# All products of x as seven block products per pair of tiles, with the work of attention and RG-LRU placed beside the gates

## The chip, the cores and the metric

One core of a Trainium2 chip. The metric is the device time of the whole kernel in microseconds (us), from a few runs. Engines are called PE (TensorE), DVE (VectorE), ACT (ScalarE), POOL (GpSimd) and SP (SyncE, which issues the DMAs).

## The reference

One layer of a streaming encoder on x of 1024 tokens x 1024 channels, float32:

```
h = x @ w_in                                  # 46 column tiles of 128
y_a = rglru(conv(xa)) * gelu(ya)              # 8 tiles of h
y_b = b_gate * conv(c_gate * xh)              # 12 tiles
y_c = rwkv7(z)                                # 14 tiles: r, k, v, two low-rank inputs, one gate input
y_d = chunk_attention(q, k, v, rel_bias)      # 12 tiles, 8 heads of 64
merged = sum over n of sigmoid(x @ w_gate[n] + b_gate[n]) * (y[n] @ w_branch[n])   # 32 gate tiles
x = layer_norm(ALPHA * x + merged @ w_out)
ff = square(relu(x @ w_ff1)) @ w_ff2
x = layer_norm(ALPHA * x + ff + (p @ w_ple) * sigmoid(x @ w_ple_gate + b_ple_gate))
```

## The kernel before, in words

**Arithmetic.** Operands are split into a high and a low part of a reduced type. Gemm.split casts on ACT (line 347, the high part) and subtracts on DVE (line 348, the low part). Gemm.acc issues three matmuls per 128 rows of the contraction, high x high, low x high and high x low (lines 367, 368, 369), each 128x512 into a bank of PSUM.

**Products of x.** gemm_x makes one column tile: Gemm.load fetches its weights as one [128, 1024] tile and splits them in two halves; for each half of the tokens 8 x 3 matmuls run, so 48 per tile. x is split once, at the start (xh, xl). Its users are generators: zc_tile (RWKV inputs, stored to zs in DRAM), qkv_tile (stored to qkv), lru, sconv, and gate or spill (tanh of a gate tile; spill also stores it to gsd). ff1 and the embedding's gate already run in another form, seven, after combine has built sums of the blocks of x1: two column tiles are taken as a 2 x 2 block product of seven block products (12 matmuls each), with the sums of weight blocks on POOL (lines 1074, 1097, 1098).

**Order.** Instructions are recorded in the order of the code; work under tc.high_priority is moved ahead. The RWKV part is a chain of 16 units (two halves of the channels, 8 chunks of 128 tokens), Rwkv.unit, each a long sequence of small matmuls with an eviction or an elementwise step between them: pn, pq, ptm, ptv, pw, then pt and py in turn (lines 231 and 246, the copy YT on ACT between them), p12, px, pss, pp, po. After each unit, run(oth, n) records n half tiles of other products (NO = 5 per unit, NOB = 6 for the first), which fill PE between the steps; issue_after holds them behind the mark of a unit LAG = 2 back. A unit loads its inputs from zs into zt (line 115, 10 x 128 columns, two buffers); "inv" on ACT (line 128) is among the first to read it.

lru and sconv lie among these fillers. After the units come three spilled gates, then for n = 0 to 3 the gates and branch products, with attend giving steps of attention at high priority: one beside a gate already in gsd, three beside a gate computed there, times NA = 1.6. One step of attention is 14 small matmuls (scores p, transposes pt, values po), two reductions on DVE (lines 761, 766), an exponential (line 771) and copies on ACT (line 783). Then w_out with the first norm, x1_transposed and combine, the embedding, ff1, and ff2 with the last norm.

## Time and profile before

| | |
|---|---|
| runs | 2408.91, 2410.81, 2416.87 us; median 2410.81 |
| profiled execution | 2414.82 us, its span 2413.0 us |
| PE, DVE, ACT, POOL busy | 98%, 56%, 35%, 14% of the span |
| matmuls | 12114 |
| mean granted clock of PE | 0.99 |
| stages, by their first matmul | the units' step p12 (line 259) from 225 (unit 0) to 977 us (unit 15), branches and attention from 1041, w_out from 1514, x1 transposed and combined from 1580, embedding 1623, ff1 1740, ff2 2053 to the end |

A row of the windows view gives for a stretch the busy time of each engine with its count of instructions, the granted clock of PE, the busy share of the DMA engines and what they moved. Starts and durations of matmuls overlap in the records, so the number of matmuls in a window says more than their busy time. A row of the groups names line, engine, operation, output and inputs, shapes and count, then busy time and the mean of one in ns, then the idle time ahead of them and what ended it.

### The profile page before, as it was taken

What the parts mean: (1) busy time and instruction counts of PE and PEld (TensorE: products, weight loads), DVE (VectorE), ACT (ScalarE), POOL (GpSimd) and SP (SyncE); (2) the same over time, 40 slices, a digit from 0 to 9 for tenths busy, and PEclk for the clock granted to TensorE, in tenths of its full rate; (3) what the DMA queues carried; (4) which work ended last, traced back from release to release, by engine and by line L of the source; (5) the groups of instructions that cost most, each with busy time, mean ns of one, the idle gap of its engine ahead of it and who ended that gap; (6) DMA issues with size and microseconds to landing.
All of it is one profiled execution on the core that took longest, in us unless ns stands there. A gap on an engine that the chain in (4) does not pass through costs nothing.

```text
span 2413.0 us, 31988 instructions
## 1 busy us (share of the span) xinstructions
PE 2369.2 (98%) x12114; PEld 1951.1 (81%) x12114; DVE 1353.1 (56%) x2758; ACT 845.9 (35%) x1478; POOL 345.2 (14%) x310
## 2 busy tenths in 40 slices
PE   9999999999999999999999999997999999999998
PEld 7888788777777778878888888876888888888886
DVE  5354545677677642245534334777644444776667
ACT  5543322424334222234434343334344444321110
POOL 0000100010000100000211100114145555000001
PEclk9999999999999999999999999998999999999999
DMA  5532222112121112254512224401123333532311
GB/s 200 192 126 70 88 71 70 56 53 66 53 71 53 64 60 77 98 174 125 158 53 73 80 76 142 164 31 57 44 96 111 112 114 130 187 123 89 103 53 70
DMA packets 123850, 231.33 MB, mean 96 GB/s; under 512 B 20016, under 2 KB 51888, under 8 KB 123696
## 3 DMA queue, kind: packets, MB, share of 16 engines
q1 hardware_dynamic: 123696, 229.29, 28.4%
q8 instruction: 95, 1.56, 0.3%
q14 instruction: 59, 0.48, 0.1%
HBM read 169.48 MB, written 59.77 MB: 95 GB/s over the span
## 4 chain that ended last, share of the span: by engine, by line
PE 91%; DVE 3%; DMA 3%; ACT 1%; issue 1%; POOL 0%; SPq 0%; DVEq 0%; ACTq 0%; POOLq 0%
PE f L368 5%; PE f L367 5%; PE f L369 5%; PE ggt L368 4%; PE ggt L369 4%; PE ggt L367 4%; PE af L369 2%; PE af L368 2%; PE af L367 2%; PE gc L368 2%; PE gc L369 2%; PE gc L367 2%; PE br L369 2%; PE br L367 2%; PE br L368 2%; PE gd L367 2%
## 5 line engine op out<-in xcount | busy, mean ns | idle before, releaser
L369 PE MATMUL ggt<-xh,wlgt 128*128 128x512 f32 x512 | 202.5, 396 | 0.0
L367 PE MATMUL ggt<-xh,whgt 128*128 128x512 f32 x512 | 202.4, 395 | 0.0
L368 PE MATMUL ggt<-xl,whgt 128*128 128x512 f32 x512 | 202.2, 395 | 0.0
L1183 DVE TENSOR_TENSOR x<-x,f 128x512 f32<-128x512 f32 x240 | 159.1, 684 | 74.1 <-PE f L369 73.4
L368 PE MATMUL f<-w2l,a2h 128*128 128x512 f32 x512 | 200.0, 391 | 0.0
L369 PE MATMUL f<-w2h,a2l 128*128 128x512 f32 x512 | 199.7, 390 | 0.0
L367 PE MATMUL f<-w2h,a2h 128*128 128x512 f32 x512 | 198.0, 390 | 0.0
L367 PEld LDWEIGHTS f<-w2h,a2h 128*128 128x128 f32 x512 | 96.0, 188 | 21.0 <-ACT w2h L347 0.3
L368 PEld LDWEIGHTS f<-w2l,a2h 128*128 128x128 f32 x512 | 96.1, 188 | 20.6
L369 PEld LDWEIGHTS f<-w2h,a2l 128*128 128x128 f32 x512 | 96.1, 188 | 20.6
L369 PEld LDWEIGHTS ggt<-xh,wlgt 128*128 128x128 f32 x512 | 96.2, 188 | 19.1 <-issue 0.5
L368 PEld LDWEIGHTS ggt<-xl,whgt 128*128 128x128 f32 x512 | 96.3, 188 | 19.0 <-issue 0.3
L367 PEld LDWEIGHTS ggt<-xh,whgt 128*128 128x128 f32 x512 | 96.3, 188 | 18.3
L367 PE MATMUL br<-yh,whwb 128*128 128x512 f32 x256 | 101.8, 398 | 3.2 <-ACT tg L413 1.8
L232 ACT ACTIVATE YT<-pt 128x512 fp32r<-128x512 f32 x96 | 56.8, 594 | 128.2 <-PE pt L231 126.0
L369 PE MATMUL br<-yh,wlwb 128*128 128x512 f32 x256 | 101.5, 396 | 0.1
L348 DVE TENSOR_TENSOR wlf<-wff,whf 128x512 fp32r<-128x512 f32 x80 | 65.7, 822 | 62.8 <-ACT whf L347 62.7
L368 PE MATMUL br<-yl,whwb 128*128 128x512 f32 x256 | 100.9, 394 | 0.0
L347 ACT ACTIVATE a2h<-a2f 128x1024 fp32r<-128x1024 f32 x32 | 34.0, 1061 | 177.9 <-PE f L368 109.4
L348 DVE TENSOR_TENSOR wlgt<-wfgt,whgt 128x512 fp32r<-128x512 f32 x64 | 46.8, 731 | 86.7 <-ACT whgt L347 84.5
L347 ACT ACTIVATE whf<-wff 128x512 fp32r<-128x512 f32 x80 | 50.6, 632 | 117.8 <-PE af L368 49.6
L369 PE MATMUL gc<-xh,wlc 128*128 128x512 f32 x224 | 88.1, 394 | 0.0
(490 smaller groups left out, 5962.6 us busy)
## 6 DMA issues: line engine op xcount, KB each, us to landing
wfgt<-w_gate SPq DMA_DIRECT2D x32, 512.0 KB, 3.3
wff<-w_ff SPq DMA_DIRECT2D x32, 512.0 KB, 3.3
a2f<-actd SPq DMA_DIRECT2D x32, 512.0 KB, 3.2
w2f<-w_ff SPq DMA_DIRECT2D x32, 512.0 KB, 3.9
gsd<-tg SPq DMA_DIRECT2D x44, 256.0 KB, 2.0
tl<-gsd SPq DMA_DIRECT2D x44, 256.0 KB, 3.1
zt<-zs SPq DMA_DIRECT2D x16, 640.0 KB, 4.9
qk<-qkv SPq DMA_DIRECT2D x64, 128.0 KB, 2.7
```

What stands on the lines that cost most here:

```text
L232: A.activation(dst, heads(p), AF.Copy)
L347: s.nc.scalar.activation(hi, src, AF.Copy)
L348: s.nc.vector.tensor_tensor(lo, src, hi.bitcast(F32), op=ALU.subtract)
L367: mm(ps, lh, rh, start=first and i == 0, stop=False, **kw)
L368: mm(ps, lh, rl, start=False, stop=False, **kw)
L369: mm(ps, ll, rh, start=False, stop=last and i == n - 1, **kw)
L1183: V.tensor_tensor(x1[i][:, sl], x1[i][:, sl], p, op=ALU.add)
```

## The change

1. seven now serves all 39 pairs of column tiles of x besides ff1 and the embedding. Its weights arrive as four [128, 512] blocks (pool wq, six buffers) plus one block of room for a sum. The three sums and one addition more per pair run on DVE, in place, for ff1 as well (POOL before); the combinations of x1's blocks too. The square of ff1's output moves from POOL to ACT.
2. At the start x is read as four blocks of 512 x 512; blocks(step) builds the splits of 11, 21, N2, N1, T3, 22 and N4 (N1 = 11 - 12 and so on), and the pairs of tiles 12/13, 0/1, 4/5 and 8/9 take their seven steps together, each step with the eight banks of PSUM between them. The low-rank products follow, then the units.
3. Beside the units run the other RWKV inputs, q, k and v, the inputs of LRU and short convolution (stored to hd in DRAM) and gate pairs, NO = 8 block products per unit, NOB = 10 for the first. All gates are stored to gsd. Three PSUM tags of the unit move to its own alternating bank; zt, bk and wm have one buffer (two before), gg two (three).
4. LRU and short convolution, with 1024-column operations, run after the units: beside each NX = 2 block products of the remaining gates one step of them and one of attention. The branches follow in the order 2, 1, 0, 3; each tile of the first three gives NA = 1 step of attention, and what is left of attention comes before branch 3.

The core of the diff:

```
...
-    BUFS = {t: 2 for t in ("ar", "bk", "bkT", "AA", "Qs", "TTf", "W", "SV", "bv", "D", "zt", "gn", "wm")}
-    BUFS["gg"] = 3
+    BUFS = {t: 2 for t in ("ar", "bkT", "AA", "Qs", "TTf", "W", "SV", "bv", "D", "gn", "gg")}
...
+        a11, a12, a21, a22, s1 = ws
+        def product(src, n, p, x, first=True):
+            wh = wp.tile([128, 512], F32R, tag="wh", name=f"wh{name}{n}")
+            wl = wp.tile([128, 512], F32R, tag="wl", name=f"wl{name}{n}")
+            gm.split(src, wh, wl)
+            gm.acc(p, [(wh[:, k * 128:k * 128 + 128], wl[:, k * 128:k * 128 + 128]) + XB[x, k] for k in range(4)], first, skip_group_check=not first)
...
+        def sums():
+            add(s1, a21, a22)
+            add(a21, a11, a21)
+            add(a11, a11, s1)
...
+        def p6():
+            product(a11, 3, t["a"], "N2", False)
+            kept("u2", t["a"])
+
+        def p5():
+            t["b"] = bank(bb, f"b{name}")
+            product(s1, 4, t["b"], "N1")
+            kept("p5", t["b"])
+
+        def p7():
+            product(a21, 5, t["a"], "T3", False)
+            V.scalar_tensor_tensor(t["p5"], t["a"], -1.0, t["p5"], op0=ALU.mult, op1=ALU.subtract)
+            done(1, 1, t["p5"], 0)
+
+        def p3():
+            product(a12, 6, t["b"], "22", False)
+            add(t["u2"], t["b"], t["u2"])
+            done(0, 1, t["u2"], 0)
+
+        def p4():
+            product(a22, 7, t["a"], "N4", False)
+            done(1, 0, t["a"], -1)
...
+    PAIRS = (12, 0, 4, 8)
...
+    def blocks(step):
+
+        if step in (0, 1, 5):
+            block(("11", "21", 0, 0, 0, "22")[step])
+        if step == 2:
+            for n, u in (("N1", "11"), ("T3", "12"), ("N4", "21")):
+                xr[n] = xr[u]
+            for k in range(4):
+                diff(xr["N1"][k], xr["11"][k], xr["12"][k])
+            xr["N2"] = [part("22", k, "h", F32, f"xN2{k}") for k in range(4)]
+            for k in range(4):
+                V.scalar_tensor_tensor(xr["N2"][k], xr["22"][k], -1.0, xr["N1"][k], op0=ALU.mult, op1=ALU.subtract)
+            block("N2")
+        if step == 3:
+            block("N1")
+            for k in range(4):
+                diff(xr["T3"][k], xr["22"][k], xr["12"][k])
+        if step == 4:
+            for k in range(4):
+                V.scalar_tensor_tensor(xr["N4"][k], xr["N2"][k], -1.0, xr["21"][k], op0=ALU.mult, op1=ALU.subtract)
+            block("T3")
+        if step == 6:
+            block("N4")
...
+    lock = []
+    for n, (i, bb) in enumerate(zip(PAIRS, ((0, 1), (2, 3), (4, 5), (6, 7)))):
+        ws = [W0[n][q] for q in ("11", "12", "21", "22", "s1")]
+        lock.append(seven(XA, ws, f"c{i}", zc_done(i, tmp), lambda name, n=n: kept_at[name[:2]](n), *bb))
+    for step in range(7):
+        blocks(step)
+        for g in lock:
+            next(g)
+    banks["three"] = True
+    low_rank(sg)
...
+    def others():
+        for i in (2, 6, 10):
+            yield from zc_pair(i)
+        for j in (0, 2):
+            for i in range(3):
+                yield from qkv_pair(i, j)
+        for j in (0, 2):
+            for n in (0, 4, 12, 16, 8):
+                yield from hd_pair(n + j)
+        for g in range(0, 32, 2):
+            yield from gate_pair(g)
...
+                run(NO if len(marks) > N0 else NOB)
...
+    def others2():
+        for j in range(4):
+            yield from sconv(j)
+            yield from lru(j)
+
+    lr = others2()
+    left = True
+    while left:
+        for _ in range(NX):
+            left = next(oth, None)
+        next(lr, None)
+        attend(1)
+    for _ in lr:
+        pass
...
+    def gated(n, j):
+
+        ts = [tmp(f"tl{n}{j}{h}") for h in range(2)]
+        for h, t in enumerate(ts):
+            SY.dma_start(t, gsd[n * 8 + j, :, h * 512:h * 512 + 512])
+        attend(NA)
+        return ts
+
+    for n in (2, 1, 0, 3):
...
-            s1 = total(1, a21, a22, ALU.add)
-            s2 = total(2, s1, a11, ALU.subtract)
...
-            G.tensor_tensor(s3, a11, a21, op=ALU.subtract)
-            G.tensor_tensor(s4, a12, s2, op=ALU.subtract)
...
-                G.tensor_tensor(t, t, t, op=ALU.mult)
...
+            A.activation(t, t, AF.Square)
...
```

How instructions move, at three places. First DVE near the start. Before, its first rows split the weights of tiles 12 and 13 (wlc) and the eight tiles of x (xl) in turn:

```order
L348 TENSOR_TENSOR wlc_105<-wfc_97,whc_104 128x512
L348 TENSOR_TENSOR xl_111<-xf_108,xh_110 128x1024
L348 TENSOR_TENSOR wlc_116<-wfc_98,whc_115 128x512
L348 TENSOR_TENSOR xl_134<-xf_131,xh_133 128x1024
L348 TENSOR_TENSOR wlc_139<-wfc_97,whc_138 128x512
L348 TENSOR_TENSOR xl_157<-xf_154,xh_156 128x1024
L348 TENSOR_TENSOR wlc_162<-wfc_98,whc_161 128x512
L491 MEMSET zr_329 128x1
```

With the change this is the piece in which the first split of "N2" weights stands (the first wlc below, for the pair 12/13; 59 operations of 511 or 512 columns stand ahead of it):

```order
L432 TENSOR_TENSOR w11c_138<-w11c_138,sums 128x512
L432 TENSOR_TENSOR w12c_130<-w12c_130,w11c_126 128x512
L432 TENSOR_TENSOR w12c_132<-w12c_132,w11c_134 128x512
L643 SCALAR_TENSOR_TENSOR zd_409<-z_407,mu,zd_409 128x511
L342 TENSOR_TENSOR wlc_447<-w11c_126,whc_446 128x512
L342 TENSOR_TENSOR wlc_468<-w11c_134,whc_467 128x512
L432 TENSOR_TENSOR w11c_142<-w11c_142,w1c_144 128x512
L432 TENSOR_TENSOR w12c_136<-w12c_136,w11c_138 128x512
L342 TENSOR_TENSOR wlc_489<-w11c_138,whc_488 128x512
L432 TENSOR_TENSOR w12c_140<-w12c_140,w11c_142 128x512
```

Sums of weights (line 432), token shifts (line 643) and splits (line 342) of the four pairs stand in one row on DVE; the products of "N2" wait for the splits.

Second, PE in the first RWKV unit. Before (gc are products of x, the others steps of unit 0):

```order
L368 MATMUL gc_1436<-xl_157,whc_1402 128x512
L369 MATMUL gc_1436<-xh_156,wlc_1403 128x512
L367 MATMUL gc_1436<-xh_179,whc_1402 128x512
L182 MATMUL pbg_0_1027<-rk_0_1024,cst 128x256
L195 MATMUL pq_0_1033<-ar_0_1016,bk_0_1017 128x128 x4
L368 MATMUL gc_1436<-xl_180,whc_1402 128x512
L369 MATMUL gc_1436<-xh_179,wlc_1403 128x512
L367 MATMUL gc_1436<-xh_197,whc_1406 128x512
```

With the change, from the first step of the unit on:

```order
L147 MATMUL pn_0_1181<-cst,sq_0_1179 128x2 x2
L191 MATMUL pq_0_0_1216<-ar_0_1199,bk_0_1200 128x128 x4
L178 MATMUL pbg_0_1210<-rk_0_1207,cst 128x256
L203 MATMUL ptm_0_1233<-ident,bh_0_1230 128x128 x4
L191 MATMUL pq_0_0_1217<-ar_0_1199,bk_0_1200 128x128 x4
L208 MATMUL ptv_0_1240<-ident,vs_0_1165 128x128 x2
L215 MATMUL pw_0_1245<-SV_0_1239,AA_0_1214 64x64 x8
L227 MATMUL pt_0_1259<-ident,YT_0_1256 128x128 x4
L147 MATMUL pn_1_1690<-cst,sq_1_1688 128x2 x2
L242 MATMUL py_0_1267<-Yo_0_1265,YT_0_1256 128x64 x4
L191 MATMUL pq_0_1_1725<-ar_1_1708,bk_1_1709 128x128 x4
L227 MATMUL pt_0_1274<-ident,Y_0_1258 128x128 x4
```

Before, 10 to 35 products stand between two steps; now 203 matmuls of units 0 and 1 follow each other with none between them.

Third, PE near the end of attention. Before, attention's steps (p, po) between products of a gate (ggt):

```order
L750 MATMUL p_3_0_10876<-kh_10433,q_10432 128x256
L750 MATMUL p_3_0_10876<-kl_10434,q_10432 128x256
L368 MATMUL ggt_11800<-xl_198,whgt_11796 128x512
L369 MATMUL ggt_11800<-xh_197,wlgt_11797 128x512
L367 MATMUL ggt_11800<-xh_215,whgt_11796 128x512
L368 MATMUL ggt_11800<-xl_216,whgt_11796 128x512
L369 MATMUL ggt_11800<-xh_215,wlgt_11797 128x512
L367 MATMUL ggt_11800<-xh_233,whgt_11796 128x512
L368 MATMUL ggt_11800<-xl_234,whgt_11796 128x512
L369 MATMUL ggt_11800<-xh_233,wlgt_11797 128x512
L367 MATMUL ggt_11800<-xh_251,whgt_11796 128x512
L786 MATMUL po_7_1_10683<-vt_9806,PT_7_1_10673 128x64 x5
```

With the change, behind the last product of the last gate (agt):

```order
L362 MATMUL agt_12359<-xN4l_845,whgt_12555 128x512
L363 MATMUL agt_12359<-xN4h_844,wlgt_12556 128x512
L912 MATMUL p_1_0_11291<-kh_10803,q_10802 128x256
L912 MATMUL p_1_0_11291<-kl_10804,q_10802 128x256
L948 MATMUL po_4_1_10997<-vt_9885,PT_4_1_10987 128x64 x5
L912 MATMUL p_7_1_11061<-kh_10192,q_10191 128x384
L912 MATMUL p_7_1_11061<-kl_10193,q_10191 128x384
L948 MATMUL po_5_1_11078<-vt_9885,PT_5_1_11068 128x64 x5
L944 MATMUL pt_6_10_11133<-ident,S_6_1_10974 128x128 x4
L944 MATMUL pt_6_1512_11139<-ident,S_6_1_10974 128x128
L912 MATMUL p_2_0_11354<-kh_10803,q_10802 128x256
L912 MATMUL p_2_0_11354<-kl_10804,q_10802 128x256
```

From here 215 matmuls of attention follow with no product among them, to the first of branch 2.

## Rows read from the trace of the kernel before

**Rows 1.** The page: busy engines; the chain that ended last, by engine.
```profile
PE 2369.2 (98%) x12114; PEld 1951.1 (81%) x12114; DVE 1353.1 (56%) x2758; ACT 845.9 (35%) x1478; POOL 345.2 (14%) x310
...
PE 91%; DVE 3%; DMA 3%; ACT 1%; issue 1%; POOL 0%; SPq 0%; DVEq 0%; ACTq 0%; POOLq 0%
```
**Rows 2.** Windows, ff1: us, PE busy (x), PEld, DVE, ACT, POOL, PEclk, DMA share, GB/s.
```profile
1920.00:1980.00 60.00, 60.00 (x266) 49.70 (x265) 27.33 (x31) 25.81 (x44) 34.38 (x27) 1.00 0.31 110
```
**Rows 3.** Groups: one of the three lines of the gates' products.
```profile
L367 PE MATMUL ggt<-xh,whgt 128*128 128x512 f32 x512 | 202.4, 395 | 0.0
```
**Rows 4.** Start: windows, the timeline's first cast, groups of a split.
```profile
0.00:25.00 25.00, 22.45 (x89) 15.87 (x90) 16.48 (x34) 14.66 (x20) 1.91 (x15) 1.00 0.86 313
0.00:75.00 75.00, 72.45 (x310) 57.21 (x311) 35.56 (x80) 39.32 (x61) 1.91 (x15) 1.00 0.54 193
...
3.87 0.63 ACT L347 ACTIVATE whc<-wfc 128x512 fp32r<-128x512 f32 x1 [1.86 <-DMA wfc<-w_in]
...
L348 DVE TENSOR_TENSOR wlc<-wfc,whc 128x512 fp32r<-128x512 f32 x28 | 19.3, 690 | 29.2 <-ACT whc L347 25.7 <-PE gl L540 3.5
L347 ACT ACTIVATE whc<-wfc 128x512 fp32r<-128x512 f32 x28 | 17.5, 627 | 22.0 <-PE gc L368 19.4 <-DMA wfc<-w_in 2.3 <-DVE lv L564 0.3
```
**Rows 5.** RWKV: windows of two unit ends, after one, the stage; timeline; DMA issue.
```profile
285.70:303.70 18.00, 15.21 (x113) 12.71 (x112) 12.07 (x31) 6.90 (x14) 2.37 (x3) 0.92 0.35 104
792.80:802.30 9.50, 8.72 (x76) 7.06 (x75) 8.65 (x18) 4.06 (x8) 2.57 (x3) 1.00 0.27 82
...
300.00:310.00 10.00, 9.72 (x39) 8.29 (x39) 2.72 (x6) 0.63 (x2) 0.00 (x0) 0.66 0.01 2
310.00:315.00 5.00, 5.00 (x29) 3.90 (x28) 0.42 (x1) 1.19 (x2) 0.00 (x0) 1.00 0.15 56
...
302.00:817.00 515.00, 506.22 (x2970) 407.21 (x2969) 342.22 (x799) 183.31 (x327) 44.52 (x63) 0.99 0.19 61
...
299.15 0.51 ACT L128 ACTIVATE inv<-zt,cb 128x256 f32<-128x256 f32 x1 [3.51 <-DMA zt<-zs]
...
300.19 0.49 PE L252 MATMUL py<-idr 128*128 128x512 f32 x1 [2.18 <-ACT YT L232]
...
zt<-zs SPq DMA_DIRECT2D x16, 640.0 KB, 4.9
```
**Rows 6.** Groups on DVE: attention's step, the LRU's convolution, splits of y.
```profile
L761 DVE CUSTOM_DVE_ANT_0 S<-p,bt 128x256 f32<-128x256 f32 x56 | 23.6, 422 | 3.0 <-PE pt L782 1.5 <-issue 0.3
...
L590 DVE SCALAR_TENSOR_TENSOR xc<-xa,pv,xc 128x512 f32<-128x512 f32 x24 | 18.5, 773 | 0.3
L787 DVE TENSOR_SCALAR ot<-po,sm 128x64 f32<-128x64 f32 x64 | 18.0, 281 | 42.4 <-PE po L786 42.0
L766 DVE CUSTOM_DVE_ANT_0 S<-p,msk 128x384 f32<-128x384 f32 x32 | 17.7, 553 | 7.7 <-PE p L750 7.0
...
L772 DVE RECIPROCAL sm<-sm 128x1 f32<-128x1 f32 x64 | 10.3, 162 | 31.9 <-ACT S L771 31.4
...
L348 DVE TENSOR_TENSOR yl<-yf,yh 128x1024 fp32r<-128x1024 f32 x15 | 20.1, 1337 | 22.9 <-ACT yh L347 22.9
```
**Rows 7.** Windows of attention: all work, products on line 369 alone, and 60 us of it.
```profile
1077.00:1464.00 387.00, 385.42 (x2149) 333.01 (x2148) 168.91 (x517) 160.85 (x338) 45.74 (x32) 1.00 0.30 96
...
1077.00:1464.00 387.00, 159.19 (x405) 76.01 (x404) 1.00 0.30 96
...
1320.00:1380.00 60.00, 60.00 (x329) 51.62 (x328) 19.39 (x60) 20.68 (x45) 8.86 (x6) 1.00 0.19 64
```
**Rows 8.** Groups: the same split in ff1, of loaded weights and of POOL's sums.
```profile
L348 DVE TENSOR_TENSOR wlf<-wff,whf 128x512 fp32r<-128x512 f32 x80 | 65.7, 822 | 62.8 <-ACT whf L347 62.7
...
L348 DVE TENSOR_TENSOR wlf<-S1f,whf 128x512 fp32r<-128x512 f32 x16 | 24.9, 1558 | 16.5 <-ACT whf L347 16.5
```
**Rows 9.** Window: the entry into attention.
```profile
1036.00:1052.00 16.00, 12.66 (x49) 9.29 (x48) 7.04 (x20) 6.67 (x14) 0.00 (x0) 0.89 0.58 177
```
**Rows 10.** Building the blocks of x1: window, and the chain's longest piece there.
```profile
1624.00:1656.00 32.00, 17.76 (x46) 12.45 (x45) 26.88 (x34) 16.87 (x30) 20.77 (x8) 0.63 0.17 62
...
1624.49 9.41 POOL x1R L1037
```

More of the change, by code (lines that the diff above doesn't have):

```diff
@@ L1004, in trunk @@
[L1004 to L1023 removed]
+                if kind < 2:
+                    z = rw("bkT", f"lz{kind}{h}", F32)
+                    for o in (0, 64):
+                        SY.dma_start(z[o:o + 64, :], zw[kind * 64:kind * 64 + 64, sl])
+                else:
+                    z = d[h]
@@ new lines, in trunk, with run @@
+    banks["three"] = True
[11 more added lines that the diff above has]
+            yield from gate_pair(g)
+    oth = others()
+    def run(n):
+        for _ in range(n):
+            if next(oth, None) is None:
+                return
@@ new lines, in trunk @@
+    marks = []
+    for hf in range(2):
+        R.start_half(hf)
+        for b in range(8):
+            with tc.high_priority(HP):
+                marks.append(R.unit(hf, b))
+            with ExitStack() as after:
+                if len(marks) > max(LAG, L0):
+                    after.enter_context(tc.issue_after(marks[-1 - LAG]))
+                run(NO if len(marks) > N0 else NOB)
+    mxs.close()
+    del banks["three"]
+    banks["q"] = [2, 5]
+    es = ctx.enter_context(ExitStack())
@@ new lines, in trunk, with attentions, attend @@
+    heads = []
+    def attentions():
+        heads.append(head(0))
+        for j in range(4):
+            yield from attention(j)
+    att = attentions()
+    def attend(n):
+        with tc.high_priority(HP):
+            for _ in range(n):
+                next(att, None)
+    def others2():
+        for j in range(4):
+            yield from sconv(j)
[7 more added lines that the diff above has]
+        attend(1)
@@ L1024, in combine, with places, two, each @@
+    for i in range(4, 8):
+        x1_transposed(i)
+    def places():
+        for k in range(8):
+            yield "s1", k
+            yield "s2", k
+        for k in range(4):
+            yield "s3", 2 * k + 1
+            yield "s5", 2 * k + 1
+    pl = places()
+    def two():
+        return next(pl), next(pl)
+    def combine():
+        def each(f):
             for kp in range(2):
                 for c in range(2):
-                    V.tensor_tensor(raw[kp, 0][:, c, :], raw[kp, 1][:, c, :], raw[kp, 0][:, c, :], op=ALU.subtract)
@@ L1193, in _pack @@
+    g2, b2_ = row(2, 0, "g2"), row(3, 1, "b2r")
+    groups = [[f, f + 1] for f in range(0, 28, 2)] + [[28, 29, 30, 31]]
+    for n, fs in enumerate(groups):
+        feed2(n, fs, last=n == len(groups) - 1)
 def _pack(i):
```

1332 lines of the change are left out of this document (639 added, 693 removed).

## The prediction, before the change was run

> **What bounds the kernel now.** I read the page first: TensorE (PE) is busy nearly the whole span, holds 91% of the chain that ended last, and no other engine comes near [rows 1]. Such a share says nothing of stages, so next came the windows. In the ff1 stage 60 us hold 266 matmuls of 128x512 and nothing else [rows 2]: 0.2256 us each, the price of one more or one fewer where PE has work waiting. (The mean that the groups give, 395 ns, overlaps its neighbours [rows 3].) Then I looked for windows with fewer. Four places stand out: the first 25 us, where products wait for data [rows 4]; the last steps of the RWKV units [rows 5]; the entry into attention [rows 9]; and the building of the blocks of x1, 32 us in which PE runs 46 matmuls [rows 10]. Everywhere else a product removed is time removed, as long as the engines that feed PE keep up.
>
> **The removal.** There are 78 column tiles of x, at 48 matmuls; the 32 gate tiles show it, 512 matmuls on each of three lines [rows 3]. As 39 pairs of seven block products of 12 they need 84 instead of 96 per pair: 39 x 12 = 468 fewer, at 0.2256 us -105.6 us. ff1 and the embedding had this form before and don't gain.
>
> **The start, +25.** Each split costs DVE 690 ns and ACT 627 ns [rows 4], and now x is split in seven blocks rather than once, four pairs need their sums, and sixteen differences of blocks of x come on top. By the order, DVE has 59 operations of 512 columns ahead of the split of the first "N2" weights. Its first 12 can follow the loads; the rest run from about 17.3 us (16 loads of 256 KB, 4.2 MB, at 313 GB/s [rows 4] from 3.9 us, when the first piece landed [rows 4]), so 47 x 0.69 = 32 us later, at 50 us. PE has until then only 2 x 48 matmuls, 21.7 us, done at about 36 us as their own splits come. It waits some 14 us, has 240 matmuls left, 54 us, and with a few us at the lower clock ends the four pairs at 106 us. At full rate 336 matmuls are 75.8 us: 30 us lost. Before, the first 75 us hold 310 matmuls, ten of them warming up [rows 4]: 75 - 300 x 0.2256 = 7 lost. I take +25, bounds +15 (sums hidden behind products) and +38 (DVE at 0.82 us, as for wlf [rows 8]).
>
> **RWKV, +16.** The last steps of a unit run without products between them already: 18.0 us for 113 matmuls at worst, 9.5 us for 76 at best [rows 5], 0.16 and 0.125 us each. With products between them the others cost, in the attention stage, (387 - 1215 x 0.2256)/934 = 0.121 us [rows 7]. So such a step costs 0.03 to 0.04 us per matmul above its work. By the order PE now has fillers of 96 per unit for 120, and two changes follow. First, units 0 and 1 run 203 matmuls with no product at all, where before each of their steps had some 20 behind it: 203 x 0.04 = +8. The eight products of the gate's low-rank weight before them share one bank, and each waits for its eviction (0.6 us [rows 4], about what it needs itself): +6. Second, the later stretches hold 673 instead of 788 small matmuls: 115 x 0.035 = -4. Then zt, bk and wm have one buffer: the load of a unit's zt, 4.9 us, can be issued only when the unit before has read it. ACT already waits 3.51 us for it at 299 us with two buffers, and the copy YT that PE needs stands behind it on ACT: PE idles 2.18 us [rows 5]. On SP weights for the fillers stand behind a zt load that waits. Fifteen units, most of the wait beside products: +6. Bounds of the whole: -4 (every wait covered) and +45.
>
> **Gates beside attention and LRU, +5.** Per two block products (24 matmuls, 5.4 us) and one attention step (14 matmuls x 0.121 = 1.7 us) PE needs 7.1 us. DVE has 2/7 of a pair's 14 operations, 4 x 0.7 = 2.8 us, the step's reductions and scalings, 0.42 + 0.55 + 0.28 + 0.16 [rows 6] and 0.4 for its smallest = 1.8, and 1.6 of LRU or short convolution (0.77 per 512 columns [rows 6]): 6.2 us, 87%. That fits with little slack; 0 to +25.
>
> **The dry end of attention, +32.** The gates now run out before attention does. By the order, after the last gate product PE has 215 small matmuls of attention without a single product, until the first of branch 2, whose inputs need memory that the gates' pools and LRU held. Beside products those 215 would be 215 x 0.121 = 26 us. DVE's order between the two holds 61 us: 17 steps x 1.5 = 26 us, sixteen operations of 1024 columns of the LRU, the convolution and the splits of y, at 1.3 to 1.6 us about 24 (four splits yl are 1.34 each [rows 6]), and 11 of smaller ones. ACT is not fuller. DVE sets the end: 61 - 26 = 35, and I take +32 since it can work ahead of PE at the rim. Before, the same steps lay beside gate products with PE at 60.00 of 60 us and DVE at 19.4 [rows 7]: the cover is what is removed. Bounds +15 and +55 (the steps in sequence, lower clock). A second stretch of 43 matmuls before branch 1 waits for a load of y, for which I take the 4.9 us of zt [rows 5]: +5, 0 to +8.
>
> **What goes away, -12.** At the entry into attention 16 us hold 49 matmuls; at the stage's 2149/387 = 5.55 per us they would hold 89 [rows 7, 9], and 40 x 0.18 = 7 us are lost. Gate products now run there: -6, 0 to -8. At the blocks of x1 PE runs 46 of 142 matmuls that 32 us hold: 21 us lost, with POOL's 9.41 us the longest piece of the chain, and DVE slowed beside it (wlf 1558 beside POOL's sums, 690 ns else) [rows 8, 10]. All differences go to DVE, eight more of 0.69, "N2" is ready some 17 us after the last copy, and p1 and p2 cover 5.4 of it: some 15 lost, -6, 0 to -12. In ff1 a pair is 84 matmuls, 18.95 us; DVE with the sums has some 10 of it and ACT with the squares 11: nothing, in either direction. The order has 276 more DMAs of 256 KB and 76 fewer of 512 KB (gates and the inputs of LRU and convolution go to DRAM and back, weights come in quarters), some 33 MB more, and 296 more ACT operations of 512 columns, 0.63 us each, 186 us. Both lie beside products: the DMA engines are 19% busy beside the units [rows 5], ACT 35% overall [rows 1]. If that cover goes, it shows as a wait for zt or for weights, which the upper bounds above hold.
>
> **The sum.** -105.6 + 25 + 16 + 5 + 32 + 5 - 6 - 6 = -34.6 us. The profiled execution took 2414.8 us (span 2413.0, 1.8 outside), so 2380.2; it lies 4.0 above the median of the runs, so **2376 us**. Most of the removal is given back because products that covered DVE's work are what is removed.
>
> **Rivals.** (A) *The stalls are covered*: the engines work ahead of PE by the buffers, and only the start and a third of the dry end stay. -105.6 + 25 + 11 - 12 = -82: about 2329. For it: DVE is 56% and ACT 35% busy overall. Against it: the order shows the bare stretches, and nothing can be moved into them. (B) *Every unit of RWKV restarts PE at the half clock*. The wait for the single zt stands in front of YT on ACT in each unit, and PE falls as it did after 297 us: 2.18 us idle, then 39 matmuls in 10 us at a granted clock of 0.66, where the next 5 us hold 29 at 1.00 [rows 5]: 19 of 58 missing, 3.3 us. With the 2.18 that is 5.5 us per unit, 15 x 5.5 = 82 in place of the +6: the sum is +41, about 2452. It decides from 2.7 us per unit on ((34.6 + 6)/15). For it: with two buffers it was seen once in full. Against it: over the whole stage, 515 us, the clock was 0.99 [rows 5]. The Trainium skill ("TensorE: Matmul & The Clock Gate", section "HAM oscillation — how this bites in real kernels") says that where bursts of matmuls alternate with waits, each burst starts throttled anew, so that the cost is paid per burst and not once. By that rule every dry end would pay; the row for the stage disagrees for the kernel before, whose ends were dry too but short of idle time. (C) *DVE bounds gates, attention and LRU*: if its operations there take 0.82 us for 0.69, as wlf in ff1 [rows 8], its 28 steps of 6.2 us become 207 us against PE's 199 and the dry end's 61 become 72: +11 there, and on the gates +8 with some +5 of waits in turn, sum about -11, 2400.
>
> **How the numbers follow.** Forecast 0.50, A 0.20, B 0.15, C 0.15. What a measurement tells from no change is 0.3%, 7.2 us: faster means under 2403.6, slower over 2418.0. Faster: 0.45 of the forecast (its bounds reach over the line at their ends), all of A, 0.08 of C: 0.73. Same: 0.03, 0.05 of C, 0.03 of B: 0.11. Slower: 0.02, 0.02 of C, 0.12 of B: 0.16. The range: A's centre at the low end, 2326, where only its better half is left out (0.09); at the high end B from 5 us per unit is left out (0.10), 2428.
>
> **What would show it.** Right: PE windows of 4 us that hold few matmuls between about 36 and 50 us; a stretch of some 60 us before branch 2 with DVE full and no product; the ends of the RWKV units at about the length of before, the first two longer; POOL gone from the chain at x1. Wrong: the branch-2 stretch shorter than 40 us (towards A), the mean clock under 0.95 from the first unit to the last (B), DVE at 95% while gates run (C), or a rate of products lower than 266 per 60 us in ff1.

## The result and the profile after

The changed kernel is slower: 2522.48 us, median of 4 runs (2519.48 to 2526.48), beside 2412.81 us (2408.91 to 2416.87, 4 runs) for the kernel before; ratio 1.0455, 95% interval 1.0429 to 1.0482. The forecast was 2376 us, the range 2326 to 2428. The profiled execution has a span of 2523.3 us, 110.3 more than before.

Three lines of the page of the changed kernel, its busy engines, the granted clock of PE in 40 slices, and the chain that ended last, answer to [rows 1]:

```profile
PE 2377.5 (94%) x11646; PEld 1942.0 (77%) x11646; DVE 1591.9 (63%) x3163; ACT 1011.4 (40%) x1789; POOL 140.7 (6%) x167
...
PEclk8995888999899899999996899999999999999999
...
PE 76%; DVE 6%; DMA 5%; ACT 3%; issue 2%; POOL 0%; SPq 0%; DVEq 0%; ACTq 0%; POOLq 0%
```

468 matmuls are gone, as the change says. But PE, 98% busy and 91% of the chain before, is 94% busy and 76% of the chain now, DMA stands in the chain with 5% (3% before), and ten of the 40 slices show clocks of 0.5 to 0.8 where before it was one:

```profile
PEclk9999999999999999999999999998999999999999
```

To see where the time went, each stretch is taken against its own work: its length less 0.2256 us for each 128x512 matmul and 0.121 us for each other, the two prices of [rows 2, 7]. What is left I call lost. The windows of the changed kernel that go with it (us, PE busy and its matmuls, PEld, DVE, ACT, POOL, clock, DMA share, GB/s):

```profile
0.00:116.10 116.10, 100.94 (x394) 77.91 (x395) 82.08 (x142) 65.22 (x119) 12.20 (x16) 0.91 0.43 142
116.10:279.80 163.70, 146.76 (x652) 118.18 (x652) 90.32 (x192) 69.05 (x130) 3.33 (x5) 0.77 0.33 107
279.80:1015.30 735.50, 686.44 (x3920) 558.68 (x3919) 464.96 (x1061) 254.81 (x498) 59.71 (x87) 0.92 0.24 73
1087.80:1317.00 229.20, 227.12 (x1182) 188.53 (x1180) 166.75 (x365) 155.15 (x279) 0.60 (x6) 1.00 0.44 143
1317.00:1397.40 80.40, 59.47 (x288) 51.23 (x288) 51.26 (x148) 48.02 (x96) 0.00 (x0) 0.65 0.38 126
...
1397.40:1625.10 227.70, 206.16 (x1000) 173.42 (x1000) 110.70 (x233) 65.00 (x121) 46.78 (x32) 0.93 0.45 143
...
1740.00:1772.00 32.00, 23.50 (x90) 17.50 (x90) 30.77 (x52) 17.82 (x31) 0.00 (x0) 0.89 0.20 66
```

Two windows of the kernel before, from its first low-rank product to step p12 of unit 1, and on to p12 of unit 15, answer to the second and third:

```profile
61.60:238.40 176.80, 176.66 (x917) 146.26 (x915) 77.36 (x176) 76.66 (x135) 3.23 (x4) 1.00 0.38 132
238.40:977.00 738.60, 726.07 (x4233) 585.55 (x4233) 440.25 (x1039) 247.66 (x450) 64.87 (x88) 0.99 0.20 65
```

Between p12 of unit 1 and of unit 15 PE runs 313 matmuls fewer, and the stretch is 735.5 us instead of 738.6. What was taken out of it came back as 49.1 us of idle time (12.5 before), and the rest as matmuls at a lower clock, 0.92 for 0.99. Lost, stage by stage, in us:

| stage | before | after | more | in the forecast |
|---|---|---|---|---|
| start, to the first low-rank product | 6 | 28 | +22 | +25 |
| low-rank products, units 0 and 1 | 0 | 46 | +46 | +14 |
| units 1 to 15 | 27 | 94 | +68 | +2 |
| to the entry into attention | 6 | 2 | -4 | -6 |
| gates beside attention and LRU | 0 | 9 | +8 | +5 |
| dry end of attention | - | 45 | +45 | +32 |
| branches | 0 | 32 | +32 | +5 |
| w_out, ff1, ff2 | 16 | 25 | +9 | 0 |
| blocks of x1, embedding | 23 | 13 | -10 | -6 |
| all | 78 | 294 | +216 | +71 |

216 less the 105.6 removed is the 110 us of the result. PE's idle time is 44 us before and 146 after, so of the 216 some 102 are idle and 114 are matmuls that took longer. The mean clock tells the second part over again: 0.990 of 2413 us before, 0.938 of 2523 after, 132 us of full rate more that were not granted (idle time at the lower clock counted in).

Two views show the waits. In the timeline of the changed kernel at 585 us, inside the units (start, duration, engine, line, operation, idle time before it and its releaser):

```profile
583.86 1.91 PE L250 MATMUL py<-Y,AA 128*128 128x128 f32 x8
...
585.62 0.42 DVE L142 TENSOR_TENSOR kk<-zt,pv 128x256 f32<-128x256 f32 x1 [0.89 <-DMA zt<-zs]
585.62 0.51 ACT L123 ACTIVATE dec<-zt,cb 128x256 f32<-128x256 f32 x1 [3.59 <-DMA zt<-zs]
...
586.90 0.68 DVE L252 TENSOR_TENSOR R<-py,Y 128x512 fp32r<-128x512 f32 x1
...
587.64 0.66 PE L255 MATMUL p<-YT,R 128*128 128x128 f32 x4 [1.44 <-DVE R L252]
```

ACT waits 3.59 us for the zt of the next unit. The unit that is ending needs R for p12. The product py that R reads ended at 585.77 us, but R starts on DVE only at 586.90, behind the first steps of the next unit (kk and what follows it), and PE waits 1.44 us for it. The wait of ACT is not new: before, it was 3.51 us long where [rows 5] show it. The list of waits from 238 to 1016 us (engine, line, what it waits for: us in total, times, longest) tells what is. First the kernel before, then the changed one:

```profile
ACT inv L128 <- DMA zt<-zs: 34.2, 12, 5.4
...
DVE km L164 <- DMA zt<-zs: 10.0, 5, 3.1
```

```profile
ACT dec L123 <- DMA zt<-zs: 34.4, 13, 5.6
DVE kk L142 <- DMA zt<-zs: 24.1, 14, 3.2
...
PE py L242 <- ACT YT L228: 9.6, 10, 2.3
```

ACT waits as long for zt in both. What is new is that DVE waits for it in nearly every unit, 24.1 us in 14 waits instead of 10.0 in 5, with the steps of the ending unit behind it, and that PE, with fewer products between, waits for those steps: 9.6 us for YT alone.

In the chain of the changed kernel at a change of branch (start, duration, what):

```profile
1522.48 0.24 PE br L363
1522.74 1.07 ACT yh L341
1523.83 1.44 DVE yl L342
1525.29 4.01 DMA yf<-ys
1529.39 1.06 ACT yh L341
1530.48 1.24 DVE yl L342
1531.73 2.43 DMA wfwb<-w_branch
1534.24 0.64 ACT whwb L341
1534.93 0.79 PE br L361
1535.72 0.43 PE br L362
```

From the last product of branch 1 to the first of branch 0 everything stands in one line for 12.4 us, and the next matmuls take 0.43 us each, the lower clock, instead of 0.23. The same lines stand at 1578 us. Before, products of gates lay there.

### The profile page after: what moved, and what is told of

The parts are those of the page before. It is cut to its first block, busy times and chain, and to the rows that moved or that the text cites. A ratio compares the mean times of both kernels' runs of the same rounds, so it can differ in the third digit from the quotient of the medians.

```text
span 2523.3 us, 32084 instructions
## 1 busy us (share of the span) xinstructions
PE 2377.5 (94%) x11646; PEld 1942.0 (77%) x11646; DVE 1591.9 (63%) x3163; ACT 1011.4 (40%) x1789; POOL 140.7 (6%) x167
## 4 chain that ended last, share of the span: by engine, by line
PE 76%; DVE 6%; DMA 5%; ACT 3%; issue 2%; POOL 0%; SPq 0%; DVEq 0%; ACTq 0%; POOLq 0%
PE f L363 5%; PE f L362 5%; PE f L361 5%; DMA zt<-zs 3%; PE br L361 2%; PE af L363 2%; PE br L362 2%; PE af L361 2%; PE af L362 2%; PE br L363 2%; PE agt L361 2%; PE agt L362 2%; PE agt L363 2%; PE pt L227 2%; PE ah L361 2%
## 5 line engine op out<-in xcount | busy, mean ns | idle before, releaser
L362 PEld LDWEIGHTS f<-w2l,a2h 128*128 128x128 f32 x512 | 96.0, 188 | 22.5
L341 ACT ACTIVATE whf<-wff 128x512 fp32r<-128x512 f32 x96 | 60.6, 632 | 98.7 <-PE af L362 37.3
L948 PEld LDWEIGHTS po<-vt,PT 128*128 128x128 f32 x480 | 71.4, 220 | 14.8 <-ACT yd L957 5.1
L242 PEld LDWEIGHTS py<-Yo,YT 128*128 128x128 f32 x384 | 63.6, 227 | 24.4 <-ACT YT L228 16.2
L242 PE MATMUL py<-Yo,YT 128*128 128x64 f32 x384 | 69.3, 308 | 12.5 <-ACT YT L228 9.6
L227 PE MATMUL pt<-ident,Y 128*128 128x128 f32 x384 | 73.0, 324 | 7.8 <-DVE Y L243 7.7
L948 PE MATMUL po<-vt,PT 128*128 128x64 f32 x480 | 72.1, 300 | 7.4 <-ACT yd L957 4.6
L361 PEld LDWEIGHTS br<-yh,whwb 128*128 128x128 f32 x256 | 50.0, 195 | 31.1 <-ACT whwb L341 21.2
L227 PEld LDWEIGHTS pt<-ident,Y 128*128 128x128 f32 x384 | 53.7, 166 | 18.0 <-DVE Y L243 10.1
L1102 POOL TENSOR_TENSOR mvn<-mvn,nh 128x1 f32<-128x1 f32 x16 | 14.8, 927 | 919.5 <-DVE mvn L1101 919.5
```

The lines of the kernel that those rows point to most:

```text
L227: T.transpose(p[:, h * 128:h * 128 + 128], src.bitcast(F32)[:, h, :], ident)
L242: T.matmul(p1[:, h * 64:(h + 1) * 64], YT[:, h, :], Yo[:, h * 64:(h + 1) * 64], start=True, stop=True)
L341: s.nc.scalar.activation(hi, src, AF.Copy)
L361: mm(ps, lh, rh, start=first and i == 0, stop=False, **kw)
L362: mm(ps, lh, rl, start=False, stop=False, **kw)
L948: T.matmul(po[:, 0:64], PT[:, c * 128:c * 128 + 128], vt[:, (k0 + c) * 128 + par * 64:(k0 + c) * 128 + par * 64 + 64], start=c == 0, stop= ...
```

## The experiments

Except for the last, each run is one execution, compared with the kernel before on the same chip (2409.94 us for the first four runs, then 2415.51, 2415.73, 2415.46, a median of 9, and 2415.77). Below, "over before" is that difference; for the changed kernel it is 109.7. The expectations of the later runs use rougher gains (27, 24, 13 and 27 us for 23, 27, 11 and 29 here). The kernel before alone lay between 2408.91 and 2418.19 us; some 5 us of such a difference, at worst 9, are not to be trusted. The lost time of a stretch repeats better (start 25 to 28, x1 13.0 to 13.5, ff2 16.2 to 16.7 wherever the stage was not touched; only the run with two banks for q lost 33 at the start).

**zt with two buffers again**

```
-    BUFS = {t: 2 for t in ("ar", ...)}
+    BUFS = {t: 2 for t in ("zt", "ar", ...)}
...
-TX = 7
+TX = 5
```

> The changed kernel with two buffers for zt again (the temporaries TX go from 7 to 5 to make room). In the changed kernel the load of zt lies on the chain that ended last with 3% of the span, 75 us, and the units from 1 to 15 take 735 us for 24 matmuls fewer per unit than before. Theory (the single zt makes each unit wait for its load): the step p12 of the units comes every 44 to 46 us instead of 49, and the whole falls by 50 to 75 us, to 2450 to 2475. Rival (the chain of a unit takes 49 us by itself, whatever lies beside it): the period stays at 48 to 49 us and the whole at 2510 to 2525.

2496.66 us, 86.7 over before, so 23 us better. Between units 1 and 15 the loss falls from 94 to 71.5 (clock 0.94), and zt's share of the chain there from 7.3% to 2.0% (of the chain from unit 1 to 15). The wait is real, but it is a third of the extra loss, not all of it: both theory and rival had the size wrong.

```profile
273.50:985.90 712.40, 675.13 (x3919) 549.84 (x3918) 461.44 (x1061) 253.90 (x496) 60.27 (x88) 0.94 0.24 75
```

**The kernel before with one zt**

```
-    BUFS = {... "D", "zt", "gn", "wm")}
+    BUFS = {... "D", "gn", "wm")}
```

> The kernel before with one buffer for zt instead of two, nothing else: the price of the wait alone, with 120 filler matmuls per unit. Theory (zt waits are the price): 15 units by 3 to 5 us, +45 to +75 us, 2455 to 2490, mean period 53 to 55 us, clock down to 0.95 to 0.97. Rival (the fillers of before cover such a wait): within 10 us of 2411.

2425.87 us, 15.9 over before; the units lose 41.9 instead of 26.5. That lies between the theory and the rival: the units pay 15 us where 120 fillers cover the wait, and 23 in the changed kernel, where 96 do and more stands on DVE.

```profile
237.80:991.60 753.80, 734.64 (x4233) 594.23 (x4233) 439.08 (x1041) 247.85 (x452) 62.35 (x88) 0.97 0.20 65
```

**The kernel before with 96 fillers per unit**

```
-NO = 5
+NO = 4
```

> The kernel before with 96 filler matmuls per unit instead of 120 (NO 4 for 5); what is left over runs after the units without them beside it. Theory (PE's work sets the period as long as zt has two buffers): the period of the units falls from 49.2 to 44 to 46 us and the whole stays within 15 us of 2411. Rival (the chain of steps takes 49 us by itself): the period stays at 48 to 49 us, and the fillers come on top, 11 units by 24 x 0.2256 us, about +60 us, 2470.

2427.97 us, 18.0 over before. The stretch from unit 1 to 15 shortens from 738.6 to 660.8 us, 52.8 to 47.2 us per unit (these are the mean periods; the 49 of the expectations left out the last, longer units). So the chain of steps can run faster than it did, and the rival falls; the whole missed the theory's 15 us by 3. Fewer fillers alone cost the units 15 us (41.7 lost for 26.5), not 68.

```profile
238.20:899.00 660.80, 639.50 (x3821) 519.03 (x3821) 426.32 (x1023) 226.74 (x416) 62.54 (x88) 0.97 0.19 60
```

**Fillers held back for the first units**

```
+                    s.early = T.matmul(q2[par]...
...
+                elif len(marks) > 1:
+                    after.enter_context(tc.issue_after(earlies[len(marks) - 2]))
-                run(NO if len(marks) > N0 else NOB)
+                run(NO if len(marks) > N0 else NOB if len(marks) > 1 else FIRST)
```

> The changed kernel with the fillers that are recorded after units 1 and 2 held back until the first matmul pq of units 0 and 1 (14 block products before, as many beside units 0 and 1 as the order gives). Theory (from 200 to 280 us the two units run bare at the lower clock, 46 us lost between 120 and 280 us): the loss there falls to 10 to 20 us and the whole by 25 to 35 us, to 2488 to 2500. Rival (the low-rank products, now with fewer fillers beside them, lose as much, or the fillers are missed later): within 10 us of 2522.

FIRST is 14, the block products beside the first units. 2508.91 us, 99.0 over before, 11 better. The loss around the low-rank products and the first two units falls from 46 to 37, the units after them from 94 to 80, but from attention to branch 2 it rises from 53 to 64. The theory's loss of 10 to 20 and its 25 us were not reached; the rival was right that fillers are missed later: what covers the first units is missing in part at the other end.

**The kernel before with the banks of the changed one**

```
-PB = {..., "q": 2, ...}
+PB = {..., "q": 1, ...}
...
-    PTAG = {..., "p12": "r", "po": "o", ...}
+    PTAG = {..., "p12": "r", "pbg": "r", "pq1": "r", "ptv": "r", "po": "o", ...}
...
-        q2 = [ps("pq"), ps("pq")]
+        q2 = [ps("pq0"), ps("pq1")]
```

> The kernel before with the RWKV unit's PSUM banks as in the changed kernel: one bank for q instead of two, and pq1, ptv and pbg in the unit's own alternating bank; nothing else. With 96 fillers instead of 120 the kernel before loses 15 us more between units 1 and 15, with one zt another 15; the changed kernel loses 68 more there, so some 30 are open. Theory (the shared banks put the steps of a unit behind each other's evictions): 15 to 30 us more between units 1 and 15. Rival (the banks cost nothing, the rest is DVE's queue, whose fillers' splits and sums stand before the unit's steps): within 6 us there. The low-rank products, on one bank too, then lose 5 to 10 us.

Units 1 to 15 lose 53.3 instead of 26.5, and the stretch of the low-rank products to unit 0 17.1 instead of 0.2: in the units as the theory had it, before them more. The 2558.27 us of the whole say nothing of the change, since attention and ff2 ran with one bank for q here too, which the changed kernel doesn't ask of them.

```profile
41.50:246.80 205.30, 200.72 (x927) 165.92 (x925) 75.92 (x165) 81.74 (x141) 2.37 (x2) 0.94 0.36 124
259.90:1034.50 774.60, 750.76 (x4275) 607.43 (x4274) 436.86 (x1040) 251.24 (x453) 64.69 (x88) 0.96 0.20 64
```

**Sums of weights on POOL**

```
+        def gadd(o, u, v):
+            G.tensor_tensor(o, u, v, op=ALU.add)
...
-            add(s1, a21, a22)
+            gadd(s1, a21, a22)
```

and likewise the other two sums and the addition to a12.

> The changed kernel with the four additions of weight blocks per pair on POOL, as the block products had them before; splits and the rest stay on DVE. Theory (DVE's queue delays the steps of the units and the first N2): 39 pairs by 4 x 0.69 us less on DVE; between units 1 and 15 10 to 25 us less lost, at the start 5 to 10 less, the whole 2490 to 2510. Rival (DVE's operations beside POOL's become slower, 1.56 us for 0.69 as in ff1 before, or the sums come later from POOL at 1.3 us each): no gain or up to +20 us.

2498.32 us, 82.8 over before, 27 better. The units lose 68.6 instead of 94; the start, where the first pairs' sums now come from POOL, loses 3 more. So the fillers' sums on DVE cost the units as much as the single zt. They do it as a queue: from 238 to 1016 us PE waits 10.8 us for steps on DVE here, 30.1 in the changed kernel and 5.1 before, for R alone 0.6 instead of 7.6. The rival's slow operations show in part. A sum mostly takes 1.3 to 1.6 us on POOL; the splits of the products beside the units take 0.68 to 0.79 (0.68 to 0.81 in the changed kernel), but those of ff1 0.86 instead of 0.69. The lines are the units' window, then PE's wait for R in the changed kernel and here:

```profile
275.40:985.30 709.90, 675.94 (x3921) 552.13 (x3920) 434.97 (x985) 253.18 (x499) 158.49 (x163) 0.93 0.24 76
```

```profile
PE p L255 <- DVE R L252: 7.6, 5, 2.6
...
PE p L255 <- DVE R L252: 0.6, 2, 0.4
```

**Six block products beside a unit instead of eight**

```
-NO = 8
+NO = 6
```

> The changed kernel with 6 block products beside each of the later units instead of 8, so that 22 block products, 264 matmuls, move behind the units to where attention runs. Theory (the products are cover that the units and attention share, and what one is given the other lacks): the period of the units falls by less than 3 us, the loss between units 1 and 15 rises by 20 to 40 us, the dry end of attention loses 15 to 40 us less, the whole stays within 20 us of 2522. Rival (the period follows the fillers, 5.4 us per unit, since zt and the banks are hidden): the loss between the units stays at about 94, the whole falls by 20 to 40 us.

2524.13 us, 108.6 over before: the same time. Units 1 to 15 take 697.0 instead of 735.5 us, 2.8 us less per unit where 5.4 of products went, and lose 115 instead of 94 at a clock of 0.87; from the first step of attention to branch 2 the loss is 36 instead of 53. As the theory had it, units and attention share one stock of products, and it is too small for both.

```profile
277.30:974.30 697.00, 660.94 (x3656) 534.94 (x3655) 437.93 (x1021) 226.81 (x451) 57.46 (x87) 0.87 0.22 68
1049.80:1401.10 351.30, 336.10 (x1741) 280.81 (x1740) 244.46 (x562) 229.71 (x422) 0.60 (x6) 0.95 0.43 141
```

**Memory of their own for the inputs of branches 1 and 3**

```
-            yh = slot("s4", 2 * k, ...)
+            yh = slot(*(("s1", k + n // 2 * 4) if n % 2 else ("s4", 2 * k)), ...)
```

and yl in the same way with "s2".

> The changed kernel with the split inputs of branches 1 and 3 in memory of their own (free until w_out), so that they needn't wait for the last product of the branch before; nothing else. In the changed kernel PE idles 20 us between 1500 and 1625 in two gaps of 10 us, each on the chain last matmul, cast, split, load of y, cast, split, load of weights, cast. Theory (that chain, bare since no gate product stands there any more): two gaps become 0 to 5 us each, the whole falls by 10 to 20 us. Rival (the two buffers that y and the weights share keep the chain): within 5 us of 2522.

2495.84 us, 80.3 over before, 29 better, more than expected. The same 1000 matmuls of the branches take 200.4 us instead of 227.7, at a clock of 0.98 for 0.93: with the two gaps the slow matmuls behind them go as well.

```profile
1395.30:1595.70 200.40, 200.07 (x999) 168.96 (x999) 111.42 (x233) 65.89 (x121) 45.88 (x32) 0.98 0.52 163
```

**Two banks for q in the changed kernel**

```
-    PTAG = {..., "pbg": "r", "pq1": "r", "ptv": "r", ...}
-    banks["three"] = True
+    banks["q"] = [2, 5]
...
```

> The changed kernel with the banks of the units as before: pq1, ptv and pbg in the two banks of q again, for which the products of x have two banks instead of three while the units run (their first block product is then kept in SBUF and added by DVE, one DVE operation more per pair). The banks alone cost the kernel before 27 us between units 1 and 15 and 17 us around the low-rank products. Theory (the banks are part of the 68 us lost more): 15 to 30 us less lost between units 1 and 15, 5 to 15 less before unit 0, the whole 2480 to 2505. Rival (the products, with two banks, now wait for their own evictions, or DVE's extra operation takes it back): within 10 us of 2522.

2503.55 us, 87.8 over before, 22 better, but in another place than expected: from the first low-rank product to unit 0 the loss falls from 44 to 16, between units 1 and 15 only from 94 to 90, while the start, and the stretch from the first step of attention to branch 2, lose 5 more each. In the units the products now have two banks and DVE an operation more per pair, which is not separated from the banks of the steps.

```profile
121.20:240.40 119.20, 114.89 (x538) 94.00 (x536) 76.69 (x160) 59.94 (x114) 2.53 (x2) 0.92 0.45 145
```

**All five together, and three of them**

The edits of zt, sums, first fillers, branch memory and banks in one kernel; then zt, sums and branch memory alone.

> The changed kernel with five of its parts undone or mended together: two buffers for zt, sums of weights on POOL, fillers held back for the first units, memory of their own for the inputs of branches 1 and 3, and two banks for q. Alone they gave 27, 24, 13 and 27 us; the banks are asked beside this. Theory (they are separate losses at different places, except that zt, sums and banks share the 68 us of the units): -27 -27 -13 and together some 45 to 60 for the units: 2395 to 2420, that is, about the kernel before. Rival (they hide behind each other): 2430 to 2460.

> The changed kernel with three of the five edits: two buffers for zt, sums on POOL, memory of their own for the inputs of branches 1 and 3. Alone they gave 27, 24 and 27 us. Theory (zt's wait and DVE's queue are separate waits of the same chain and add up): between units 1 and 15 some 45 us lost, the whole 2440 to 2450. Rival (what is too short there is the cover, 96 matmuls for 120, and each edit frees the same idle time): some 65 to 70 us lost between the units as with either alone, the whole 2460 to 2472.

2466.41 and 2469.39 us, 50.7 and 53.9 over before. For both the rivals are nearer. The branches keep their gain (2.5 and 4.4 lost), but the units lose 72 and 61 where zt or the sums alone gave 71.5 and 68.6: zt and sums together free 33 us, where 48 would be freed if they added up, and with the two banks and the held fillers besides it is 11 less. With all five the start loses 39.9. The windows are the units in the first and in the second:

```profile
281.60:989.50 707.90, 682.64 (x3896) 559.85 (x3896) 435.61 (x995) 246.55 (x479) 154.25 (x160) 0.92 0.24 75
```

```profile
275.80:980.40 704.60, 675.96 (x3941) 550.87 (x3942) 439.30 (x998) 254.68 (x496) 161.23 (x166) 0.95 0.24 76
```

**Three steps of attention in flight**

```
-DP = 2
+DP = 3
...
-TX = 7
+TX = 5
```

> The changed kernel with three steps of attention in flight instead of two (DP 3; TX 5 instead of 7 makes room, which alone left the stretch from the first attention step to branch 2 at 310 us). Theory (the dry end is bound by the latency of steps and loads one after another, DVE being 35 of 60 us busy there): the stretch falls by 8 to 25 us, the whole to 2495 to 2515. Rival (DVE's or ACT's work sets it, as predicted): within 5 us there and in the whole.

2522.47 us, 106.7 over before, and 312.9 us for 309.6 from the first step to branch 2: no gain. So it is not the number of steps in flight. The number fits the rival, but its reason does not: in the changed kernel DVE is busy for 51.26 of the 80.4 us, ACT for 48.02, and of the chain that ended last there DVE has only 10.5 us, while DMAs have 22.5, ACT 22.0 and PE 19.5. PE is busy 59.47 us with 288 matmuls that would be some 36 us at the prices above: at a clock of 0.65 the small matmuls are slower, and the rest is waits for DMAs and for steps of other engines. Which of them would have to go first, is not settled.

**120 fillers in the mended kernel**

```
-NO = 8
+NO = 10
```

> The kernel of e12 (two zt, sums on POOL, memory for branch inputs) with 10 block products beside each unit instead of 8: 120 matmuls per unit, as before the change, and 22 products fewer beside attention. Theory (the units lacked cover): the loss between units 1 and 15 falls from 61 to 30 to 45 us, that from the first step of attention to branch 2 rises from 56 by 10 to 25, the whole stays within 12 us of 2469. Rival (DVE's queue or POOL's late sums delay the units whatever the cover): the loss in the units stays at 55 to 65 us and the whole rises by 10 to 25.

The edits of zt, sums and branch memory are in it too. 2493.24 us, 77.5 over before. The loss in the units stays at 58 (61 with 96 fillers), that of attention rises from 56 to 79: the rival. Beyond zt and the sums, then, the units of the changed kernel lose some 32 us more than before for a reason that fillers don't mend. The banks are one candidate, since they alone cost the kernel before 27 us there; giving them back in the changed kernel took banks from the products, so that it doesn't decide. DVE's other additions (splits of every block, the subtractions from PSUM) and the order on SP were not tried.

```profile
277.50:1039.10 761.60, 733.92 (x4206) 599.58 (x4205) 465.13 (x1026) 279.24 (x540) 180.30 (x178) 0.95 0.25 79
```

**The kernel before with the differences of x1 on DVE**

```
-                    G.tensor_tensor(raw[kp, 1][:, c, :], raw[2 + kp, 1][:, c, :], raw[kp, 1][:, c, :], op=ALU.subtract)
+                    V.tensor_tensor(raw[kp, 1][:, c, :], raw[2 + kp, 1][:, c, :], raw[kp, 1][:, c, :], op=ALU.subtract)
```

and likewise the subtraction for "T4".

> The kernel before with the eight differences of x1's blocks that stand on POOL put on DVE, the one part of the change that takes away a wait and no cover; nothing else. Theory (POOL's 9.41 us on the chain and DVE's slower operations beside it go, as in the changed kernel, where the stage loses 13 us instead of 23): 6 to 10 us faster, 2402 to 2406, faster than both kernels. Rival (the eight operations on DVE take their place on the chain): within 3 us.

2402.34 us, median of 5 runs, beside 2415.46 (9 runs): ratio 0.9941, interval 0.9928 to 0.9955. This version is faster than both kernels. The 32 us in which PE ran 46 matmuls [rows 10] hold 88, and the stage loses 13.5 us instead of 23. The other few us of the ratio lie in differences of 1 to 3 us at several places that the edit doesn't touch.

```profile
1621.00:1653.00 32.00, 23.75 (x88) 17.78 (x87) 30.64 (x50) 19.64 (x35) 4.57 (x3) 0.84 0.19 66
```

## Why the prediction was wrong

**The removal, the start, the entry, the gates, x1: right.** 468 matmuls went, ff1 runs 263 to 267 per 60 us. At the start PE has 10 and 7 matmuls in two windows of 10 us between 30 and 50, with DVE full, as worked out:

```profile
30.00:40.00 10.00, 4.15 (x10) 2.79 (x10) 10.00 (x21) 4.32 (x9) 8.54 (x3) 0.83 0.00 1
40.00:50.00 10.00, 3.72 (x7) 2.09 (x8) 10.00 (x17) 6.10 (x14) 0.00 (x0) 0.54 0.23 88
```

22 us were lost for the +25. The gates cost 8 for +5 with DVE at 73%, not 87; x1 gave 10 for -6, and POOL left its chain.

**"203 x 0.04 = +8", and "+6" for the low-rank products: 46.** The bare stretch is there, 280 matmuls long in the trace where the order showed 203, but the price of 0.03 to 0.04 us each came from unit ends that ran at clocks of 0.92 and 1.00 [rows 5], and those two ends give 0.04 and 0.004, not 0.03 to 0.04. Here the low-rank products on their one bank (28 of the 46, by the run with two banks), the loads of zt, 6.6, 4.4 and 4.7 us on the chain, and the steps follow each other, and the granted clock is 0.50 from 200 to 270 us:

```profile
200.00:250.00 50.00, 35.94 (x128) 25.72 (x128) 25.33 (x71) 13.51 (x29) 2.09 (x2) 0.50 0.28 90
250.00:270.00 20.00, 19.96 (x93) 18.46 (x92) 9.93 (x22) 5.22 (x10) 0.00 (x0) 0.50 0.00 0
```

A price for idle time that is taken from a stretch at full clock can't be used where idle time is several times as long.

**"Most of the wait beside products: +6", and -4 for fewer bare steps: +68.** This is the step that decided; RWKV as a whole, +16 with an upper bound of +45, measured +114. The single zt is 23 us of the 68 (15 in the kernel before), the sums in DVE's queue 26, both together 33. Fewer fillers cost the kernel before 15 and its banks 27, but here neither more fillers (58 for 61) nor two banks (90 for 94) gave that back, so some 32 of the 68 stay open. I had counted the sums as nothing wherever DVE was far from full, and DVE is only 63% full between units 1 and 15. But R stood for 1.1 us behind other operations at 586 us, and in a chain of dependent steps what counts is how long a step waits behind another's operation, not how full the engine is.

**"DVE sets the end": +32, measured 45.** The dry end is there, from 1317 to 1397 us, but it is 80 us long where DVE's order held 61, with 279 small matmuls and 8 of the LRU where the order showed 215. DVE is 64% busy in it and has 10.5 us of the chain, PE is busy for 74% of it, at a clock of 0.65. The size came near; the reason given for it was wrong.

**"A load of y: +5": 32 in the branches.** I priced the one bare stretch that the order showed and did not look at the changes of branch, where before gate products stood between the last product of one branch and the first of the next. The run with memory of their own recovers 27 of them.

**The rivals.** B named the right places and the right pair, a wait on zt and a lower clock after it, and had 0.15. Between units 1 and 15 the clock did what B says: it was granted at 0.50 in 13 separate stretches, 116 us in all, near the last steps of twelve of the fourteen units (two stretches, 14 us, before). In the 6 us ahead of each fall PE idled for 0.9 to 2.9 us, mostly in waits between small matmuls. Three windows show two of the stretches (p12 of unit 7 is at 587.6 us, of unit 8 at 639.5):

```profile
580.10:586.90 6.80, 5.98 (x23) 4.92 (x23) 3.41 (x11) 1.85 (x4) 1.26 (x3) 0.50 0.48 135
586.90:631.30 44.40, 40.52 (x250) 32.25 (x250) 29.65 (x69) 15.23 (x32) 4.41 (x8) 1.00 0.28 86
631.30:638.10 6.80, 5.30 (x22) 4.65 (x23) 4.61 (x12) 3.45 (x7) 0.00 (x0) 0.50 0.03 7
```

The Trainium skill ("TensorE: Matmul & The Clock Gate", section "HAM oscillation — how this bites in real kernels") has it that with waits between bursts each burst starts throttled anew and the cost comes back every time; here the trace agrees, with 13 falls of the clock in these units, while in the kernel before, with 0.99 in the units, it could be left out. The units lost 4.8 us more each, where B had 5.5 and turned the sum from 2.7 on: with their +68 in place of +2 the sum is +31, slower already, and the low-rank products, the dry end, the branches and smaller losses made it 110. What B had wrong is the cause, which it put into zt alone: zt was 23. I had set B aside because the clock was 0.99 over the stage [rows 5], but that row was of a kernel with two buffers for zt, 120 fillers per unit and no sums on DVE. The clock was 0.92 in the units, under the 0.95 named for B, and 0.77 before them. A (everything covered) and C (DVE full beside the gates) were not seen; DVE was at 73% there. The upper end of the range, 2428, was said to leave out B from 5 us per unit; by B's own sum it leaves it out from 3.9, and 5 would be 2445. The result lies above both.

The common error is one: 468 matmuls were priced as time, and the stalls that they had covered were priced one by one where the order showed a bare row. The kernel before had 78 us lost in 2413; its products were the cover of two long chains, and the run with two block products fewer per unit shows that taking cover from one uncovers it in the other. Cover is not all of it: where zt and the sums were mended, 120 fillers for 96 gave the units only 2 us back.

## What to carry to other kernels

Where matmuls fill the gaps of chains of dependent steps, removing some is worth their time only as long as the chains still find cover; count the chains' own latency first, and the cover that is left. Price an uncovered stretch at the lower clock, and an operation added to an engine in such a chain by the steps that stand behind it, however idle the engine is on average. Of a large rewrite, the part that takes away a wait and no cover can be tried alone: here one such part, two lines, gave 0.6%.

## What the runs showed of the hardware

- PE stayed at the lower level, granted 0.50, 1.2 GHz, through 20 us in which it was busy for 19.96 with 93 matmuls of the units, all but one of at most 128 columns (250 to 270 us above). It came back before any product followed: the next 10 us, 86 more matmuls of the units, were at 0.86, and the first product started at 280.4 us.
- The split of a weight block in ff1 takes DVE 687 ns in the changed kernel, where POOL does nothing beside it, and 857 with the sums of weights back on POOL and nothing else changed. Before, it took 822 ns on the mean, 1558 for those of POOL's sums [rows 8].

The window from 250 to 270 us stands above; this is the next one, and the group of the splits in the changed kernel and with the sums on POOL (line, engine, operation, shapes, count, busy time and mean in ns):

```profile
270.00:280.00 10.00, 9.86 (x86) 8.50 (x85) 7.22 (x25) 1.87 (x5) 1.24 (x3) 0.86 0.01 2
...
L342 DVE TENSOR_TENSOR wlf<-wff,whf 128x512 fp32r<-128x512 f32 x96 | 66.0, 687 | 63.1 <-ACT whf L341 62.6
...
L342 DVE TENSOR_TENSOR wlf<-wff,whf 128x512 fp32r<-128x512 f32 x96 | 82.3, 857 | 106.6 <-ACT whf L341 106.6
```
